# Layer B's bias rows loaded and negated one head pair earlier in a two-layer hybrid encoder

## The chip, the cores and the metric

One core of one Trainium2 chip runs the whole program. The metric is the device time of one execution in microseconds (us), the median of three runs. Each profile is of one further execution. The engines are TensorE (PE, with PEld for its weight loads), VectorE (DVE), ScalarE (ACT), GpSimd (POOL) and SyncE (SP), which here only issues DMAs.

## What is computed

The reference is a two-layer encoder block on x of shape (1, 512, 1024) in float32. Each layer is a pre-norm, one wide input projection, an attention with 16 heads of 64, a product with a gate, one output projection and a residual:

```python
hn = rms_norm(x, norm_gain[i])
if i % 2 == 0:   # layer A: three dilated windows per head, merged by their denominators
    y = mixer_a(hn, a_w_in, a_w_out, a_q_gain, a_k_gain, t5_bias)
else:            # layer B: neighbourhood attention on an 8 x 64 grid with a 2-D bias b_rpb
    y = mixer_b(hn, b_w_in, b_w_out, b_q_gain, b_k_gain, b_rpb)
x = x + y
```

In layer B a query adds to its logits `rpb[head, key row - query row + 7, key column - query column + 15]`, and a column outside its window of 16 is masked. The change is about how this table comes into the form that layer B needs; all of it is done while layer A runs.

## The kernel before

**Tiling.** Everything is kept transposed, features in the 128 partitions and the 512 tokens in the free dimension. A product runs at nearly full float32 precision as three matmuls of rounded parts (`mm3`): weights and activations are each split into a high part (`wh`, `hn_h`) and the rest (`wl`, `hn_l`). A weight piece `wraw` of 128x1024 comes from DRAM by a DMA of SP (L201) into one of four buffers; ACT or DVE rounds each half of it to `wh` (L141, L143), and POOL or DVE subtracts to get `wl` (L149, in `split`). There are four buffers each of `wh` and `wl`, and a step of a projection takes twelve matmuls for each.

**Stages.** Layer A works on the heads in eight pairs, 0 to 7. For each pair `main_a` projects keys with values (`rawk`), queries with the near keys (`rawq`), near values and the gate; after it follow the output product, then layer B in the same manner. The attention of a pair runs beside the projections of later pairs, as a generator `side()` that is pumped between matmuls. It has two halves: scores on PE into `log`, softmax on DVE (L980, L992, L826) and ACT (L1003, L827), transposes on DVE (L911) and a turn through DRAM (`td`, `pt`). The second half of pair 1 thus runs while the keys of pair 3 are projected. When ACT has copied a projection out of PSUM (L555), POOL or ACT squares it (`sq`, L315 and L313), DVE sums the squares (`ss`, L316), takes a reciprocal root (L121 to L129) and scales and turns the result (L335, L592). POOL also adds the low part of the gated output (L867).

**What sets the order.** PE's order is the program's. `clock` adds up estimated PE time while the program is written, and `later_on(delay, job)` puts a job on a list by that clock, in ns; `tick()` issues what is due. The other engines' orders are fixed when the kernel is built, by a simulated timeline in which only instructions marked `keep_in_program_order` keep their place. Every engine runs its list strictly in order, and all these DMAs stand in one list on SP.

**The bias rows of layer B.** `bias_rows()` (L467) does this:

- L470 loads `rp` (128x248, one row for each head and query row) into an `eg` buffer. There are two of these; the gates of layer A use them too (L614, L820).
- On POOL, L473 fills a second `eg` buffer `lb` (128x376) with a large number, L471 negates `rp` in place, and L474 copies its middle into `lb`.
- 16000 ns later `keep` (L476) writes both to DRAM, as `gb_d` and `lb_d` (L478).
- 30000 ns after the call, and then every 10500 ns, one of fourteen DMAs in DRAM spreads these rows into `ex_d` (L492): four of 512x160 elements, then smaller ones of 512x32 to 512x128. Four last DMAs order them into `eb_d` (L496) in pairs 4 and 5. Layer B reads `eb_d` much later.

It is called in `side()` (L1392), at the end of the first half of pair 1's attention.

Of the kernel before, what the change touches and what calls it, by code (L numbers as in the profile page):

```python
# [59 lines left out]
def tile_hybrid_encoder(  # L60
# [189 lines left out]
    def later_on(delay, job):  # L250

        timers.append((clock[0] + delay, job))
        timers.sort(key=lambda t: t[0])
# [123 lines left out]
    def row_scale(ssq):  # L377

        rsqrt(nc.vector, rs_n, ssq, 4, 1.0 / D)
# [28 lines left out]
    def gains():  # L408
        nc.sync.dma_start(hg, head_gain)
        nc.gpsimd.tensor_copy(ng.rearrange("p l k -> p (l k)"), x_ng[:, : 2 * KT])  # L410
        for i, (a, b) in enumerate(((0, 3), (1, 4), (2, 5), (6, 7))):
            m = nc.vector.scalar_tensor_tensor(
                gk[:, i : i + 1], hg[:, a : a + 1], -SCALE, hg[:, b : b + 1], op0=ALU.mult, op1=ALU.mult
            )
            tc.keep_in_program_order(m)

    def scales_a():
        pa = spread()
        nc.scalar.mul(trj(rs_half), to_trj(pa), 0.5)

    def norm(layer, k, xk):

        g = (ng if layer else x_ng[:, : 2 * KT].rearrange("p (l k) -> p l k", l=2))[:, layer, k : k + 1]
        h, l = hn_h[:, k, :], hn_l[:, k, :]
        nc.scalar.activation(h, xk, AF.Copy, scale=g)
        return nc.vector.scalar_tensor_tensor(l, xk, g, h.bitcast(F32), op0=ALU.mult, op1=ALU.subtract)

    def square_a(k):
        nc.scalar.activation(x_of(k), x_of(k), AF.Square)

    def row_sums(ssq):

        pk = bank("pk")
        for t in range(4):
            matmul(pk[:, t : t + 1], ssq[:, P * t : P * t + P], ones.bitcast(F32)[:, 0:1], start=True, stop=True)
        return pk[:, 0:4]

    def bias_lines():

        t5 = wk.tile([16, LINE], F32, tag="tr", name="t5", bufs=1)  # L440
        tc.keep_in_program_order(nc.sync.dma_start(t5, t5x))
        mk = wk.tile([16, LINE], F32, tag="q12", name="mk", bufs=1)
        nc.sync.dma_start(mk, maskc)
        nc.vector.tensor_sub(mk, mk, t5)
        nc.sync.dma_start(line_d[:, :384], mk[:, :384])
        nc.sync.dma_start(lines_d.rearrange("h g c -> h (g c)"), mk[:, 384:])

        def spread_out(dst, src):
            tc.keep_in_program_order(nc.sync.dma_start(dst, src))

        line = lambda o, *dims: bass.AP(line_d.tensor, line_d.offset + o, [[448, 16], *dims])
        fars = lambda o, *dims: bass.AP(lines_d.tensor, lines_d.offset + o, [[448, 32], *dims])
        far = l12_d.rearrange("h g r c -> (h g) r c")
        jobs = [
            (l0_d[:, 32 * j + 8 * s : 32 * j + 8 * s + 8, :], line(127 - j - 4 * s, [-16, 8], [1, 256]))
            for j in range(4)
            for s in range(4)
        ]
        jobs += [
            (far[:, 8 * s : 8 * s + 8, 56 * k : 56 * k + 56], fars(64 * (3 - s + k) + 7, [-1, 8], [1, 56]))  # L460
            for s in range(4)
            for k in range(4)
        ]
        for n, job in enumerate(jobs):
            later_on(3000 + 500 * n, partial(spread_out, *job))

    def bias_rows():  # L467

        rp = wk.tile([P, 248], F32, tag="eg", name="rp")
        tc.keep_in_program_order(nc.sync.dma_start(rp, rpb))  # L470
        nc.gpsimd.tensor_scalar(rp, rp, -1.0, None, op0=ALU.mult)  # L471
        lb = wk.tile([P, 376], F32, tag="eg", name="lb")
        nc.gpsimd.memset(lb, BIG)  # L473
        nc.gpsimd.tensor_copy(lb[:, 15 * 8 : 31 * 8], rp[:, 7 * 8 : 23 * 8])  # L474

        def keep():  # L476
            for dst, src in ((gb_d, rp), (lb_d, lb)):
                tc.keep_in_program_order(nc.sync.dma_start(dst, src))  # L478

        later_on(16000, keep)  # L480

        far, near = (lb_d, 376), (gb_d, 248)
        jobs = [(2 * W5 + W5 * n, W5, far, 120) for n in range(4)]
        jobs += [(o, 32, far, 24) for o in (0, W5, 7 * W5 - 32, 8 * W5 - 32)]
        jobs += [(32, 32, near, 216), (64, 96, near, 120), (W5 + 32, P, near, 88)]
        jobs += [(6 * W5, P, near, 56), (7 * W5, 96, near, 56), (7 * W5 + 96, 32, near, 24)]

        def spread_out(o, n, src, at):
            t, width = src
            dst = bass.AP(ex_d.tensor, ex_d.offset + o, [[4 * EB, P], [EB, 4], [1, n]])  # L490
            src = bass.AP(t.tensor, t.offset + at, [[width, P], [-8, 4], [1, n]])
            tc.keep_in_program_order(nc.sync.dma_start(dst, src))  # L492

        def in_order(c):
            dst = eb_d.rearrange("h (c r) x -> c h r x", c=4)[c]
            tc.keep_in_program_order(nc.sync.dma_start(dst, ex_d[:, c].rearrange("(h r) x -> h r x", h=16)))  # L496

        for n, job in enumerate(jobs):
            later_on(30000 + 10500 * n, partial(spread_out, *job))
        st["rows"] = [partial(in_order, c) for c in range(4)]  # L500

    st = {}
# [682 lines left out]
    def residual(src, f0):  # L1185
        xs = pq.rearrange("p (k t) -> p k t", k=KT)
        st["xr"] = [xs[:, f, :] for f in range(KT)]
        for f in range(f0, f0 + 4, 2):
            nc.sync.dma_start(xs[:, f : f + 2, :], src[:, f : f + 2, :])
            yield 1000  # L1190
# [169 lines left out]
    def side():  # L1360
        for k in range(KT):
            norm(0, k, x_of(k))
            if k:
                square_a(k - 1)
            stamp["na", k] = 0
            if k == 4:
                gains()
            yield 1000
        square_a(KT - 1)
        for k in range(1, KT):  # L1370
            yield 1300
            nc.vector.tensor_add(x_of(0), x_of(0), x_of(k))
        yield 1500
        row_scale(row_sums(x_of(0)))
        yield 2500
        bias_lines()
        later_on(21000, lambda: st.__setitem__(("e", 0), bias_a(0)))
        yield 2500
        scales_a()
        first_out()  # L1380
        stamp["rs", "a"] = 0
        halves = []
        for hc in range(NHC):
            if hc < NHC - 1:
                yield from q_a(hc)
                if hc:
                    yield from halves.pop(0)
                yield from st.pop(("land", hc))()
                half = attn_a(hc)
                for v in half:  # L1390
                    if v == "half":
                        if hc == 1:  # L1392
                            bias_rows()
                        if hc in (4, 5):
                            for n in range(2):
                                later_on(9000 + 3500 * n, st["rows"].pop())
                        halves.append(half)
                        break
                    yield v
            else:  # L1400
                gap[0] = cycle((500, 500, 700))
                yield from halves.pop(0)
                yield from chain(q_a(hc), k_a(hc))
                yield from attn_a(hc)
        yield from residual(xg, 0)
        yield from residual(xg, 4)
        stamp["ya", KT - 1, "y"] = 0
        yield "wait", ("x", KT - 1), 800
        for f in range(KT):
            square_b(f)  # L1410
            yield 600
        yield 4500
        row_scale(row_sums(st.pop("ssq")))
        stamp["rs", "b"] = 0
        yield 5000
        nc.scalar.mul(rs_half, spread(), 0.5)
        stamp["rs", "all"] = 0
        for job, hc, delay in B_PLAN:
            yield "wait", ("b", "start"), delay
            if job == "scores":  # L1420
                yield from side_b(hc)
                continue
            if hc == NHC - 1:
                yield "wait", ("back", hc), 0
                yield from residual(xm_d, 0)
            yield "wait", ("back", hc), 3500
            if hc == NHC - 2:
                stamp["yb", "turned"] = 0
            pending.pop(0)()
            if hc == NHC - 1:  # L1430
                stamp["yb", "last"] = 0
            yield
            if hc == NHC - 1:
                yield from residual(xm_d, 4)

    run(main(), side())


# [101 lines left out]
```

## Time and profile before

| | |
|---|---|
| median of 3 runs | 803.38 us (802.29 to 803.6) |
| the profiled execution | 803.4 us, of which the profiled span is 801.6 us |
| PE busy | 795.8 us, 99% of the span |
| DVE, ACT, POOL busy | 66%, 55%, 28% |
| DMA | 174.76 MB, mean 218 GB/s |

The profile covers the span; 1.8 us of the execution lie around it. Its engine rows are in us from the span's start, each with the start, the length, the engine and line, the operation, the tile written and the tiles read, the count and, in square brackets, how long the engine had been idle before and what released it. Matmuls are pipelined: one of 128x512 shows 0.39 us, but they start some 0.23 us apart. PE's granted clock is full in every slice.

### The profile page before, as it was taken

What the parts mean: (1) busy time and instruction counts of PE and PEld (TensorE: products, weight loads), DVE (VectorE), ACT (ScalarE), POOL (GpSimd) and SP (SyncE); (2) the same over time, 40 slices, a digit from 0 to 9 for tenths busy, and PEclk for the clock granted to TensorE, in tenths of its full rate; (3) what the DMA queues carried; (4) which work ended last, traced back from release to release, by engine and by line L of the source; (5) the groups of instructions that cost most, each with busy time, mean ns of one, the idle gap of its engine ahead of it and who ended that gap; (6) DMA issues with size and microseconds to landing.
All of it is one profiled execution on the core that took longest, in us unless ns stands there. A gap on an engine that the chain in (4) does not pass through costs nothing.

```text
span 801.6 us, 17757 instructions
## 1 busy us (share of the span) xinstructions
PE 795.8 (99%) x6718; PEld 654.1 (82%) x6718; DVE 526.2 (66%) x1409; ACT 442.1 (55%) x933; POOL 223.2 (28%) x351
## 2 busy tenths in 40 slices
PE   9999999999999999999999999999999999999998
PEld 7888888887888888888888888888888888887887
DVE  7474575668467568468368568538655878796744
ACT  7442744744754654664564575636336666656721
POOL 3242432441532432432532322211220405120010
PEclk9999999999999999999999999999999999999999
DMA  8579577867987986986987966166546797899564
GB/s 293 153 212 259 162 224 223 249 189 232 285 258 201 274 244 197 278 264 229 270 233 249 287 199 186 31 203 228 157 147 201 208 241 217 226 253 279 154 153 176
DMA packets 97526, 174.76 MB, mean 218 GB/s; under 512 B 16608, under 2 KB 52592, under 8 KB 97440
## 3 DMA queue, kind: packets, MB, share of 16 engines
q1 hardware_dynamic: 97296, 173.36, 74.0%
q8 instruction: 53, 0.87, 0.5%
q14 instruction: 33, 0.27, 0.1%
q10 hardware_dynamic: 144, 0.26, 0.1%
HBM read 130.98 MB, written 50.86 MB: 227 GB/s over the span
## 4 chain that ended last, share of the span: by engine, by line
PE 75%; ACT 0%; DVE 0%; issue 0%
PE acc L237 66%; PE log L237 4%; PE o L237 4%; PE tp L241 1%; ACT wh L141 0%; PE pa L237 0%; PE pk L237 0%; DVE pt L1210 0%
## 5 line engine op out<-in xcount | busy, mean ns | idle before, releaser
L237 PE MATMUL acc<-wh,hn_h 128*128 128x512 f32 x704 | 278.0, 396 | 0.9 <-ACT wh L141 0.9
L237 PE MATMUL acc<-wl,hn_h 128*128 128x512 f32 x704 | 274.0, 390 | 0.9 <-POOL wl L149 0.9
L237 PE MATMUL acc<-wh,hn_l 128*128 128x512 f32 x704 | 273.8, 390 | 0.0
L141 ACT CAST wh<-wraw 128x512 fp32r<-128x512 f32 (+1 forms) x258 | 157.7, 614 | 195.9 <-PE acc L237 161.7
L149 DVE TENSOR_TENSOR wl<-wraw,wh 128x512 fp32r<-128x512 f32 (+2 forms) x187 | 136.6, 732 | 150.8 <-ACT wh L141 149.0
L237 PEld LDWEIGHTS acc<-wh,hn_h 128*128 128x128 f32 x704 | 132.6, 188 | 32.6 <-issue 3.8
L149 POOL TENSOR_TENSOR wl<-wraw,wh 128x512 fp32r<-128x512 f32 (+1 forms) x72 | 96.1, 1335 | 225.3 <-ACT wh L141 163.8
L237 PEld LDWEIGHTS acc<-wh,hn_l 128*128 128x128 f32 x704 | 132.2, 188 | 27.7
L237 PEld LDWEIGHTS acc<-wl,hn_h 128*128 128x128 f32 x704 | 132.3, 188 | 27.5 <-POOL wl L149 1.2
L315 POOL TENSOR_TENSOR sq<-rawq 128x256 f32<-128x256 f32 (+1 forms) x82 | 59.6, 735 | 124.7 <-ACT rawq L555 112.0
L237 PE MATMUL acc<-y,wh 128*128 128x512 f32 (+1 forms) x272 | 81.6, 384 | 0.0
L1003 ACT ACTIVATE p<-p,mn 128x512 f32<-128x512 f32 (+1 forms) x64 | 44.8, 702 | 62.0 <-DVE mn L992 62.0
L237 PE MATMUL acc<-hn_h,wh 128*128 128x512 f32 x192 | 76.0, 396 | 0.0
L237 PE MATMUL acc<-hn_h,wl 128*128 128x512 f32 x192 | 74.9, 390 | 0.0
L237 PE MATMUL acc<-hn_l,wh 128*128 128x512 f32 x192 | 74.9, 390 | 0.0
L316 DVE TENSOR_REDUCE ss<-sq 128x4 f32<-128x256 f32 (+1 forms) x96 | 47.6, 505 | 34.5 <-POOL sq L315 34.0
L237 PEld LDWEIGHTS acc<-y,wh 128*128 128x128 f32 x272 | 48.9, 189 | 9.2 <-issue 0.6
L237 PE MATMUL acc<-y,wl 128*128 128x512 f32 (+1 forms) x136 | 51.4, 378 | 0.0
L335 DVE TENSOR_TENSOR rawq<-rawq,rs 128x256 f32<-128x256 f32 (+1 forms) x96 | 47.0, 550 | 2.5 <-POOL rs L133 2.2
L911 DVE STREAM_TRANSPOSE tr<-p 128x512 f32<-128x512 f32 x56 | 38.9, 705 | 11.4 <-ACT p L827 11.4
L555 ACT ACTIVATE rawq<-acc,rs_n 128x512 f32<-128x512 f32 (+1 forms) x76 | 46.0, 613 | 0.5
L827 ACT ACTIVATE p<-p,mn 128x512 f32<-128x512 f32 (+1 forms) x64 | 44.4, 701 | 2.1 <-DVE mn L826 2.1
(140 smaller groups left out, 907.8 us busy)
## 6 DMA issues: line engine op xcount, KB each, us to landing
wraw<-in_w SPq DMA_DIRECT2D x120, 512.0 KB, 5.6
td<-tr SPq DMA_DIRECT2D x14, 1024.0 KB, 7.9
pt<-td SPq DMA_DIRECT2D x56, 256.0 KB, 4.6
qd<-rawq SPq DMA_DIRECT2D x7, 1536.0 KB, 7.1
qt<-qd SPq DMA_DIRECT2D x28, 384.0 KB, 6.5
tdb<-tb SPq DMA_DIRECT2D x8, 768.0 KB, 5.7
pt<-tdb SPq DMA_DIRECT2D x32, 192.0 KB, 6.0
eb<-eb_d SPq DMA_DIRECT2D x32, 160.0 KB, 4.9
```

What stands on the lines that cost most here:

```text
L141: nc.scalar.copy(h, raw)
L149: eng.tensor_sub(l, raw, h.bitcast(F32))
L237: nc.tensor.matmul(o, l, r, **kw)
L241: nc.tensor.transpose(o, i, ident)
L315: nc.gpsimd.tensor_mul(to, v, v)
L316: nc.vector.tensor_reduce(ss[:, i * ns : (i + 1) * ns], sq.rearrange("p (a b) -> p a b", b=64), axis=AX.X, op=ALU.add)
L335: m = nc.vector.tensor_mul(v, v, by)
L555: nc.scalar.activation(dst, src, AF.Copy, scale=rs_n[:, i : i + 1])
L827: nc.scalar.activation(pr, pr, AF.Copy, scale=mn[:, 3:4])
L911: nc.vector.transpose(dst, src[:, :n].rearrange(order, b=4, k=32, **({"g": 2} if apart else {})))
L1003: nc.scalar.activation(row, row, AF.Exp, bias=mn[:, 1:2], scale=-1.0, accum_out=mn[:, 2:3])
```

## The change

`bias_rows()` is no longer called at the end of the first half of pair 1, but put on the list 12500 ns after the end of the first half of pair 0. The two writes to DRAM follow 9000 ns after the call in place of 16000, and the fourteen spreading DMAs begin 74000 ns after it in place of 30000, with the same spacing. The last four are where they were. No instruction is added or taken away.

```diff
-        later_on(16000, keep)
+        later_on(9000, keep)
...
-            later_on(30000 + 10500 * n, partial(spread_out, *job))
+            later_on(74000 + 10500 * n, partial(spread_out, *job))
...
-                        if hc == 1:
-                            bias_rows()
+                        if hc == 0:
+                            later_on(12500, bias_rows)
```

PE, DVE and ACT run the same instructions in the same order as before; rows move on POOL and SP alone. The first place is POOL's list in the first half of pair 1's attention, before: `lb` and `rp` are the bias rows, `wl` the low part of weights, `sq` the squares of pair 2's queries, `y` the gated output of pair 0.

```order
L133 TENSOR_TENSOR rs<-rs,na 128x16
L149 TENSOR_TENSOR wl<-wraw,wh 128x512
L473 MEMSET lb 128x376
L471 TENSOR_SCALAR rp<-rp 128x248
L474 COPY lb<-rp 128x128
L149 TENSOR_TENSOR wl<-wraw,wh 128x512
L315 TENSOR_TENSOR sq<-rawq 128x4x4x32 x2
```

And the same place after:

```order
L133 TENSOR_TENSOR rs<-rs,na 128x16
L149 TENSOR_TENSOR wl<-wraw,wh 128x512 x2
L315 TENSOR_TENSOR sq<-rawq 128x4x4x32 x2
L149 TENSOR_TENSOR wl<-wraw,wh 128x512
L867 TENSOR_TENSOR y<-gt,y 128x512
```

The three rows are gone from between the two `wl`, so the second `wl` and the squares no longer stand behind them. The second place is POOL's list one pair earlier, in the first half of pair 0, after; before, the same rows stood there without L473, L471 and L474.

```order
L149 TENSOR_TENSOR wl<-wraw,wh 128x512
L473 MEMSET lb 128x376
L471 TENSOR_SCALAR rp<-rp 128x248
L149 TENSOR_TENSOR wl<-wraw,wh 128x512
L474 COPY lb<-rp 128x128
L315 TENSOR_TENSOR sq<-rawq 128x4x4x32 x2
L149 TENSOR_TENSOR wl<-wraw,wh 128x512 x2
```

Here they stand ahead of one `wl` and of the squares of pair 1's queries. The third place is SP's list at the same time, after: `td` is the write of the first half's weights to DRAM, `pt` the reads of it, `vd` and `vv` the near values' turn.

```order
L201 DMA wraw<-in_w 128x1024 x3
L470 DMA rp<-in_rpb 128x248
L920 DMA td<-tr 128x4x512
L201 DMA wraw<-in_w 128x1024
L924 DMA pt<-td 32x4x512 x4
L201 DMA wraw<-in_w 128x1024
L478 DMA gb_d<-rp 128x248
L478 DMA lb_d<-lb 128x376
L201 DMA wraw<-in_w 128x1024
L644 DMA vd<-vv 128x4x128
```

Before, in pair 1, the load of `rp` stood directly behind the write of `td`; now, in pair 0, it stands directly ahead of it. The two writes stood in pair 1 between the write and the reads of `qd`, the queries' turn through DRAM. They stand now among the weight loads of pair 0.

The fourteen spreading DMAs keep their order on SP but come some places earlier: the first stood in pair 1 behind the reads of `qd` and the write of `td`, and stands now between the write `vd` and the reads `vv`, ahead of the write of `qd`.

## The prediction

> **What bounds the kernel now.** The page says it in two lines:
>
> ```profile
> span 801.6 us, 17757 instructions
> PE 795.8 (99%) x6718; PEld 654.1 (82%) x6718; DVE 526.2 (66%) x1409; ACT 442.1 (55%) x933; POOL 223.2 (28%) x351
> ```
>
> PE is busy for all but 5.8 us. The change takes no work from PE, so all it can win is one of these gaps. The waits of PE and the windows say where they are:
>
> ```profile
> PE acc L237 <- ACT wh L141: 0.9, 1, 0.9
> PE acc L237 <- POOL wl L149: 0.9, 1, 0.9
> 190.00:200.00 10.00, 8.27 (x36) 6.31 (x35) 7.48 (x15) 6.29 (x13) 2.93 (x4) 1.00 0.89 260
> 220.00:300.00 80.00, 80.00 (x742) 66.10 (x741) 51.87 (x122) 45.67 (x85) 27.11 (x38) 1.00 0.85 243
> 400.00:500.00 100.00, 100.00 (x1031) 82.17 (x1014) 73.12 (x207) 59.37 (x116) 29.42 (x33) 1.00 0.79 234
> ```
>
> Each wait row has the total, the count and the longest; a window has first its length, then PE's busy time. Between start and tail there is one hole, 1.73 us between 190 and 200 us. Matmuls are drawn longer than their spacing, so its true price comes from a repeating mark: the scores of the second half of pairs 0, 1, 2 and 3 on PE.
>
> ```profile
> 121.50 0.66 PE L237 MATMUL log<-k,q 64*32 64x256 f32 x16
> 182.99 0.66 PE L237 MATMUL log<-k,q 64*32 64x256 f32 x16
> 246.77 0.66 PE L237 MATMUL log<-k,q 64*32 64x256 f32 x16
> 308.25 0.66 PE L237 MATMUL log<-k,q 64*32 64x256 f32 x16
> ```
>
> They are 61.49, 63.78 and 61.48 us apart: the hole costs 63.78 - 61.49 = 2.29 us, 0.29% of the execution. The timelines of PE and ACT show how it ends:
>
> ```profile
> 192.90 0.39 PE L237 MATMUL acc<-wh,hn_l 128*128 128x512 f32 x1
> 194.16 0.49 PE L237 MATMUL acc<-wh,hn_h 128*128 128x512 f32 x1 [0.88 <-ACT wh L141]
> 195.51 0.50 PE L237 MATMUL acc<-wl,hn_h 128*128 128x512 f32 x1 [0.85 <-POOL wl L149]
> 192.28 1.32 ACT L827 ACTIVATE p<-p,mn 128x512 f32<-128x512 f32 x2
> 193.51 2.16 ACT L141 CAST wh<-wraw 128x512 fp32r<-128x512 f32 x4
> 194.19 1.27 POOL L149 TENSOR_TENSOR wl<-wraw,wh 128x512 fp32r<-128x512 f32 x1 [1.56 <-DMA qd<-rawq]
> ```
>
> At a spacing of 0.23 us PE wanted `wh` at 193.13 and `wl` at 193.36. ACT rounds `wh` only when pair 1's softmax is through (L827), so PE gets it at 194.16, and POOL's `wl`, done at 195.46, at 195.51. The late work is the softmax. It waited for DVE, and DVE had waited for POOL:
>
> ```profile
> 167.49 1.37 POOL L471 TENSOR_SCALAR rp<-rp 128x248 f32<-128x248 f32 x1 [11.03 <-DMA rp<-in_rpb]
> 169.18 1.29 POOL L149 TENSOR_TENSOR wl<-wraw,wh 128x512 fp32r<-128x512 f32 x1
> 170.42 1.04 POOL L315 TENSOR_TENSOR sq<-rawq 128x512 f32<-128x512 f32 x1
> 171.50 1.28 DVE L316 TENSOR_REDUCE ss<-sq 128x8 f32<-128x512 f32 x2 [3.33 <-POOL sq L315]
> 187.01 0.38 DVE L980 CUSTOM_DVE_ANT_0 p<-log,e 128x256 f32<-128x256 f32 x1
> ```
>
> POOL stood 11 us at the load of `rp`, with a `wl` and the squares queued behind it. The first square came at 170.42, DVE was idle for 3.33 us, and its timeline has hardly a gap after that until the softmax at L980 in which to catch up.
>
> **The change, part by part.** *Pair 1 loses the three POOL rows.* Pair 2 is the measure of what that gives: it has the same rows in this stretch, on each engine in the same order but for two casts of ACT (below), and no `rp`.
>
> ```profile
> 228.51 1.59 POOL L149 TENSOR_TENSOR wl<-wraw,wh 128x512 fp32r<-128x512 f32 x1 [8.62 <-ACT wh L141]
> 232.00 1.04 POOL L315 TENSOR_TENSOR sq<-rawq 128x512 f32<-128x512 f32 x1 [1.90 <-ACT rawq L555]
> 248.64 0.38 DVE L980 CUSTOM_DVE_ANT_0 p<-log,e 128x256 f32<-128x256 f32 x1
> ```
>
> Against the marks (182.99 and 246.77) the first square is 14.77 us early in pair 2 and 12.57 in pair 1, 2.20 late; L980 is 1.87 us behind its mark in pair 2 and 4.02 in pair 1, 2.15 late. So without `rp` pair 1's L980 should begin at 182.99 + 1.87 = 184.86. From L980 to the cast are 193.51 - 187.01 = 6.50 us of pair 1's own order, which the change leaves: 191.36. Then `wl` on POOL ends 2.15 us earlier, at 193.31, against 193.36 wanted. The stall just goes, with no margin; I leave 0.1 us of it. Its bounds are nothing gained, if L980 does not move, and 2.29. I take 2.2, since pair 2 is the same work.
>
> *Pair 0 gets them.* What counts is when `rp` lands. It is issued between these two:
>
> ```profile
> 100.19 0.33 SPq L201 DMA_DIRECT2D wraw<-in_w  x1
> 100.77 0.38 SPq L920 DMA_DIRECT2D td<-tr  x1
> wraw<-in_w SPq DMA_DIRECT2D x1, 512.0 KB, 4.3
> rp<-in_rpb SPq DMA_DIRECT2D x1, 124.0 KB, 7.7
> td<-tr SPq DMA_DIRECT2D x1, 1024.0 KB, 10.9
> ```
>
> The last three give the size and the time to landing: of that weight load, of `rp` before, directly behind a `td` of 1 MB, and of the slowest `td` of this stretch, issued at 196.09. Issued at about 100.6, `rp` now has only the weight load ahead, so it should land soon after 100.19 + 4.3 = 104.5: I take 104.9, between 104.5 and 100.6 + 7.7 = 108.3. POOL and DVE have there:
>
> ```profile
> 106.74 1.04 POOL L315 TENSOR_TENSOR sq<-rawq 128x512 f32<-128x512 f32 x1 [2.18 <-ACT rawq L555]
> 111.16 0.69 DVE L149 TENSOR_TENSOR wl<-wraw,wh 128x512 fp32r<-128x512 f32 x1 [0.17 <-ACT wh L141]
> 113.45 0.76 DVE L631 TENSOR_TENSOR vv<-acc,rs_half 128x448 f32<-128x448 f32 x2 [0.61 <-PE acc L237]
> 128.90 1.30 POOL L149 TENSOR_TENSOR wl<-wraw,wh 128x512 fp32r<-128x512 f32 x1 [0.34 <-DMA qd<-rawq]
> 131.64 0.39 PE L237 MATMUL acc<-wh,hn_h 128*128 128x512 f32 x1
> ```
>
> After the landing come 1.37 for the negation, 1.29 for the `wl` that now stands behind it and 0.3 for the copy to `lb`, 2.96 together: the first square starts at about 107.9 in place of 106.74, 1.1 us late. Its cover: DVE's idle 0.17 and 0.61 on the way, and at the end `wl` ready at 130.20 where PE asks for it one matmul after 131.64, at 131.87, 1.67 us. That is 2.45 us in all, so pair 0 costs nothing while `rp` lands before 106.74 + 2.45 - 2.96 = 106.2. At 108.3 it would cost 2.1 us. The `wl` behind the negation is not the first to be missed: with four buffers it is made about three steps of twelve matmuls, 8 us, ahead of its use.
>
> [...]
>
> ```profile
> 111.77 0.17 DVE L121 TENSOR_SCALAR nv<-ss 128x32 f32<-128x32 f32 x1
> 175.20 1.56 DVE L121 TENSOR_SCALAR nv<-ss 128x32 f32<-128x32 f32 x1
> 175.13 1.59 POOL L867 TENSOR_TENSOR y<-gt,y 128x512 fp32r<-128x512 f32 x1 [0.51 <-ACT y L864]
> ```
>
> So a DVE instruction can lose 1.4 us to a POOL instruction. [...] The trace agrees: the long row ends at 176.76, POOL's at 176.72. [...]
>
> *The DMAs.* Their count is the same. The two writes to DRAM no longer follow `qd` in pair 1; in pair 0 they go out among weight loads. The fourteen spreading DMAs come a few places earlier on SP. In the two full windows quoted first they ran at many places and PE missed nothing, so I put 0. The gate of pair 1 takes the buffer of `rp` again and must now wait until that is written out:
>
> ```profile
> 115.55 0.87 SPq L644 DMA_DIRECT2D vd<-vv  x1
> 135.87 0.68 DVE L613 TENSOR_TENSOR gt<-gt,rs_half 128x512 f32<-128x512 f32 x1
> ```
>
> The write stands ahead of `vd` on SP; with 7.7 us to land, as `rp` had, it is out by 123.3, and ACT writes that buffer after L613, at 136.5: 0.
>
> *Sum.* 803.4 - 2.2 + 0 = 801.2 us, of which 1.8 us lie outside the span. The profiled execution equals the median of 803.38, so the forecast stands for the median too. About 0.2%, 1.6 us, is what a measurement of this kernel can tell from no change, so that faster means below 801.8.
>
> **The rivals.** *Part of the stall stays.* The margin is 0.05 us, because in pair 1's order on ACT both last L827 stand ahead of the cast, where pair 2 has casts between them, and that order does not change. If DVE gains not 2.15 but 0.5 to 1.5 us, 0.6 to 1.6 us of stall remain: 801.8 to 802.8, no difference to be told. For: ties of DVE with POOL as above may fall otherwise. Against: pair 2.
>
> *It does nothing.* The lag of pair 1 comes from elsewhere and `rp` only happened to stand there: 803.4. Against: first square and L980 are late by the same amount.
>
> *The stall moves to pair 0.* `rp` lands 7 to 7.7 us after its issue, held up by the `td` that starts 0.2 us behind it: 1.4 to 2.1 us come back, 802.6 to 803.3.
>
> *Slower.* The same place, with a landing like the slowest `td`: 10.9 us, at 111.5. The first square would be 111.5 + 2.96 - 106.74 = 7.7 us late, PE would lose 7.7 - 2.45 = 5.3, and the time would be 803.4 - 2.2 + 5.3 = 806.5. It decides at a landing after about 110.1, 9.5 us after issue, where the loss passes 2.2 + 1.6. Against: that `td` had four reads of `qd` ahead of it; here the weight load of 4.3 us is all.
>
> **How the numbers follow.** Chances: the forecast 0.67, part of the stall 0.17, nothing 0.04, moved to pair 0 0.07, slower 0.05. The forecast's own range is 800.9 to 801.7. The range given goes from 800.8 to 802.8: it takes in the first two, 0.84, and leaves out the others. Of the forecast 0.02 may fall short of 1.6 us: faster 0.65, same 0.02 + 0.17 + 0.04 + 0.07 = 0.30, slower 0.05.
>
> **What would show it.** Right: no hole in PE between 190 and 200 us; marks 61.5 us apart for pairs 1 and 2; L980 of pair 1 some 1.9 us behind its mark; POOL's negation at about 105 and the first square of pair 0's stretch before 109.2. Wrong in pair 1: L980 still 3 us or more behind its mark. Wrong in pair 0: a hole in PE at about 131.6 with L471 later than 106.2. A new hole elsewhere, behind a weight load delayed by an `ex_d`, would make the zero for the DMAs wrong.

## The result, and the profile after

The changed kernel takes 801.35 us (median of 12 runs, 801.1 to 802.38) where the kernel before takes 803.5 us (12 runs beside it, 802.29 to 804.89). The ratio is 0.9973 with a 95% interval of 0.9964 to 0.9982: faster by 0.27%, some 2.15 us. The forecast was 801.2 us.

The profiled execution of the changed kernel took 802.38 us, the slowest of the twelve; its page begins like that of before:

```profile
span 800.6 us, 17757 instructions
PE 795.9 (99%) x6718; PEld 653.9 (82%) x6718; DVE 526.8 (66%) x1409; ACT 442.3 (55%) x933; POOL 222.2 (28%) x351
```

PE does the same 795.9 us of work, but its gaps are now 800.6 - 795.9 = 4.7 us in place of 5.8. The waits of PE (total, count, longest) and the windows say which one went:

```profile
PE busy L401 <- DVE warm L390: 0.9, 1, 0.9
PE o L237 <- DVE mn L826: 0.6, 1, 0.6
190.00:200.00 10.00, 10.00 (x45) 8.04 (x45) 5.09 (x8) 5.88 (x12) 3.20 (x4) 1.00 0.72 169
400.00:500.00 100.00, 99.44 (x1012) 81.58 (x1011) 72.34 (x202) 58.84 (x114) 29.28 (x33) 1.00 0.79 230
```

The two waits on `wh` and `wl` at 193 to 195.5 us are gone, and the window from 190 to 200 is full. A small one is new, at 463 us; the run `again` below deals with it. The same repeating marks as before, the scores of the second half of pairs 0 to 3:

```profile
121.58 0.66 PE L237 MATMUL log<-k,q 64*32 64x256 f32 x16
183.08 0.66 PE L237 MATMUL log<-k,q 64*32 64x256 f32 x16
244.75 0.66 PE L237 MATMUL log<-k,q 64*32 64x256 f32 x16
306.25 0.66 PE L237 MATMUL log<-k,q 64*32 64x256 f32 x16
```

They are 61.50, 61.67 and 61.50 us apart, against 61.49, 63.78 and 61.48. The middle distance lost 2.11 us, which is the result but for some hundredths. The first did not grow: pair 0 pays nothing for what it took over. The middle one is still 0.17 us longer than its neighbours, and PE's timeline shows where:

```profile
193.22 0.39 PE L237 MATMUL acc<-wh,hn_h 128*128 128x512 f32 x1
193.47 0.50 PE L237 MATMUL acc<-wl,hn_h 128*128 128x512 f32 x1
193.80 0.39 PE L237 MATMUL acc<-wh,hn_l 128*128 128x512 f32 x1
```

The matmul that needs POOL's `wl` starts 0.25 us after the one ahead of it, and the next 0.33 us after that, in place of 0.23 each. The last matmul of the old stall had the same look (0.50 long, the next one 0.34 behind it). So a rest of the stall is still there, too short for the list of waits.

The timelines of POOL, DVE and ACT show pair 1 after:

```profile
164.83 1.59 POOL L149 TENSOR_TENSOR wl<-wraw,wh 128x512 fp32r<-128x512 f32 x1 [8.62 <-ACT wh L141]
168.32 1.04 POOL L315 TENSOR_TENSOR sq<-rawq 128x512 f32<-128x512 f32 x1 [1.90 <-ACT rawq L555]
169.39 1.44 DVE L316 TENSOR_REDUCE ss<-sq 128x8 f32<-128x512 f32 x2 [1.13 <-POOL sq L315]
184.94 0.38 DVE L980 CUSTOM_DVE_ANT_0 p<-log,e 128x256 f32<-128x256 f32 x1
190.22 1.32 ACT L827 ACTIVATE p<-p,mn 128x512 f32<-128x512 f32 x2
191.44 1.65 ACT L141 CAST wh<-wraw 128x512 fp32r<-128x512 f32 x3
192.12 1.29 POOL L149 TENSOR_TENSOR wl<-wraw,wh 128x512 fp32r<-128x512 f32 x1 [1.57 <-ACT wh L141]
```

POOL's idle time of 11.03 us on the load of `rp` is gone. What it waits for now is the queries themselves: 1.90 us, ended by ACT's copy out of PSUM, the very bracket that pair 2 showed before. From there every row is some 2.1 us earlier against the mark: the first square 14.76 ahead of it in place of 12.57, L980 1.86 behind it in place of 4.02, the cast 8.36 behind it in place of 10.52.

Pair 0 after, on SP, POOL and DVE; the fourth row is the load's size and its time to landing:

```profile
100.26 0.33 SPq L201 DMA_DIRECT2D wraw<-in_w  x1
100.64 0.42 SPq L470 DMA_DIRECT2D rp<-in_rpb  x1
101.16 0.38 SPq L920 DMA_DIRECT2D td<-tr  x1
rp<-in_rpb SPq DMA_DIRECT2D x1, 124.0 KB, 4.5
105.25 0.83 POOL L471 TENSOR_SCALAR rp<-rp 128x248 f32<-128x248 f32 x1 [7.23 <-DMA rp<-in_rpb]
106.05 1.29 POOL L149 TENSOR_TENSOR wl<-wraw,wh 128x512 fp32r<-128x512 f32 x1
107.28 0.76 POOL L474 COPY lb<-rp 128x128 f32<-128x128 f32 x1
108.00 1.04 POOL L315 TENSOR_TENSOR sq<-rawq 128x512 f32<-128x512 f32 x1
```

POOL stands here too, for 7.23 us, and the first square begins at 108.00. Measured from the issue of the weight load (100.26, before 100.19) that is 7.74 us, against 106.74 - 100.19 = 6.55 before: 1.19 us late, and no gap in PE follows.

### The profile page after: what moved, and what is told of

Its sections match the earlier page's. It is cut to its first block, busy times and chain, and to the rows that moved or that the text cites. A ratio compares the mean times of both kernels' runs of the same rounds, so it can differ in the third digit from the quotient of the medians.

```text
span 800.6 us, 17757 instructions
## 1 busy us (share of the span) xinstructions
PE 795.9 (99%) x6718; PEld 653.9 (82%) x6718; DVE 526.8 (66%) x1409; ACT 442.3 (55%) x933; POOL 222.2 (28%) x351
## 4 chain that ended last, share of the span: by engine, by line
PE 90%; DVE 5%; DMA 3%; ACT 2%; issue 1%; ACTq 0%; SPq 0%
PE acc L237 79%; PE log L237 4%; PE o L237 4%; DMA vv<-vd 1%; DVE rawq L335 1%; DMA bd<-rawq 1%; PE tp L241 1%; DVE wl L149 1%; DMA wraw<-in_w 1%; PE busy L401 1%; ACT wh L141 0%; ACT p L1300 0%; DVE na L128 0%; ACT p L1305 0%; DVE rawq L592 0%
```

## The experiments

**Theory W**, the prediction's: the 2.1 us are the wait of POOL at the load, with the squares of pair 2 queued behind it; in pair 0 the same wait is covered. **Rival D**: what counts are the DMAs that left pair 1, above all the two writes behind `qd`. **Rival R**: the work of the three rows itself counts in pair 1, through POOL's time or through DVE held up beside it.

**`rows_only`.** From the kernel before. The load goes to pair 0, into a buffer of its own. `bias_rows` is still called in pair 1, so that the two writes and the spreading DMAs stay there; POOL's rows go to pair 0 with the load, by the order that is fixed when the kernel is built (the negation runs at 105.00).

```diff
+    def load_rows():
+        st["rows6"] = slot(6, "rows6", F32)
+        st["rp"] = st["rows6"][:, :248]
+        tc.keep_in_program_order(nc.sync.dma_start(st["rp"], rpb))
...
-        rp = wk.tile([P, 248], F32, tag="eg", name="rp")
-        tc.keep_in_program_order(nc.sync.dma_start(rp, rpb))
+        rp = st["rp"]
-        lb = wk.tile([P, 376], F32, tag="eg", name="lb")
+        lb = st["rows6"][:, 256:632]
...
+                        if hc == 0:
+                            later_on(12500, load_rows)
```

> The load of rp and the three POOL rows go to pair 0 as in the changed kernel; the two writes of gb_d and lb_d and the fourteen spreading DMAs stay where the kernel before has them (the rows stand in a buffer of their own, so that no gate waits for it). Theory W (POOL's wait at the load of rp, with the squares behind it, made pair 1's softmax late): 801.2 to 801.5 us, the whole gain, pair 1's mark to pair 2's mark 61.5 to 61.7 us. Rival D (the DMA traffic around the queries' turn in pair 1, the two writes behind qd, made it late): 803.4, marks 63.8 apart, L980 of pair 1 still about 4 us behind its mark.

801.26 us (5 runs; ratio 0.9968, 0.9956 to 0.9981). The marks stand 61.49, 61.71 and 61.49 apart. The whole gain is there with the DMAs at their old places: D falls.

**`ahead`.** From the kernel before. Everything stays in pair 1; the load alone is issued some 9 us earlier, ahead of one weight load and of `td`, and the POOL rows stand one `wl` further ahead. The delays are raised so that the later DMAs keep their places.

```diff
                 later_on(7000 + 2000 * u, send)
+                if hc == 1 and u == 0:
+                    later_on(6990, bias_rows)
...
-        later_on(16000, keep)
+        later_on(19200, keep)
...
-            later_on(30000 + 10500 * n, partial(spread_out, *job))
+            later_on(33200 + 10500 * n, partial(spread_out, *job))
...
-                        if hc == 1:
-                            bias_rows()
```

> Nothing leaves pair 1: only the load of rp goes ahead of one weight load and of the write of td, and POOL's three rows ahead of one more wl; every DMA after it stands as in the kernel before. Theory W: rp lands near 156 to 160 us, POOL is through with its rows before the next weights are cast at 164.6, the first square comes near 168.3 and the stall is gone: 801.2 to 801.6 us. Rival R (the work of the three rows in pair 1, or POOL and DVE blocking each other there): stays at 803 or above. Rival D: 803.4.

801.22 us (5 runs; ratio 0.9967, 0.9954 to 0.9979), marks 61.49, 61.72 and 61.49 apart. POOL's timeline in pair 1:

```profile
157.54 0.83 POOL L471 TENSOR_SCALAR rp<-rp 128x248 f32<-128x248 f32 x1 [6.43 <-DMA rp<-in_rpb]
168.13 1.04 POOL L315 TENSOR_TENSOR sq<-rawq 128x512 f32<-128x512 f32 x1 [1.90 <-ACT rawq L555]
```

POOL still stands 6.43 us at the load, and the rows still cost POOL their time in pair 1, but the wait is over 10 us before the queries arrive. R falls, and with it any need to leave pair 1. What counted before was when POOL was through with all that stood ahead of the squares. By pair 2's measure the squares of pair 1 could start 14.77 us ahead of the mark, at 168.22. The wait ended at 167.49, a little earlier, but the negation, the copy and the `wl` queued behind it took 2.93 us more, until 170.42.

**`wait_more`.** From the kernel before, with a copy of 0.5 MB within DRAM put ahead of the load, to make the wait longer.

```diff
+        tc.keep_in_program_order(nc.sync.dma_start(dr.tile([P, 1024], F32, name="dum"), w[:, :1024]))
         tc.keep_in_program_order(nc.sync.dma_start(rp, rpb))
```

> The kernel before with one more DMA, 0.5 MB from DRAM to DRAM that nothing reads, directly ahead of the load of rp; all orders else the same. Theory W: rp lands 2 to 4 us later than 167.5 and the stall grows by as much, since pair 1 has no cover left: 805 to 808 us, the hole in PE near 193 us grows to 4 to 6 us in the distance of the marks. Rival D, and the view that rp only happened to stand there: within 0.5 us of 803.4.

805.66 us (10 runs, 803.4 to 807.31; ratio 1.0025, 1.0011 to 1.0039). POOL's negation came only some 1.4 us later against the mark, and the first square (171.06, mark 182.73) 0.90 later than before, so the dose was smaller than meant. The price was larger: the marks are 66.07 us apart, 2.29 more than before. PE's timeline, a matmul of the usual look behind it, and two windows (the third figure from the end is PE's granted clock):

```profile
194.71 0.50 PE L237 MATMUL acc<-wh,hn_h 128*128 128x512 f32 x1 [1.68 <-ACT wh L141]
196.06 0.79 PE L237 MATMUL acc<-wl,hn_h 128*128 128x512 f32 x1 [0.85 <-POOL wl L149]
196.66 0.63 PE L237 MATMUL acc<-wh,hn_l 128*128 128x512 f32 x1
199.47 0.40 PE L237 MATMUL acc<-wh,hn_h 128*128 128x512 f32 x1
193.00:197.00 4.00, 1.47 (x4) 1.01 (x4) 3.24 (x5) 3.22 (x6) 2.08 (x3) 0.85 0.76 207
197.00:201.00 4.00, 4.00 (x14) 3.13 (x13) 1.24 (x1) 0.59 (x1) 0.69 (x1) 0.72 1.05 230
```

The first of the two idle times grew from 0.88 to 1.68 us, by 0.8, about the 0.9 us of the later square, as W has it. The rest is the clock: between 196.66 and 199.22 the matmuls take 0.63 us and start 0.43 apart in place of 0.23, that is, at about half speed (granted clock 0.85 and 0.72 in the two windows), and the windows lose 4 x 0.15 + 4 x 0.28 = 1.7 us (2.5 together, a little over the 2.29 of the marks). No theory had this. The ten runs divide in the same way: the three at a mean clock of 1.000 took 803.4 to 804.26 us, the seven at 0.996 to 0.998 took 805.4 to 807.31. So W's sign and its first 0.8 us held, and that the median lies in the expected 805 to 808 us is luck: the clock made up for the dose that was too small.

**`wait_pair0`.** From the changed kernel, with a DMA of 4096 single elements ahead of the load.

```diff
+        some = bass.AP(w.tensor, w.offset, [[w.ap[0][0], P], [2, 32]])
+        tc.keep_in_program_order(nc.sync.dma_start(dr.tile([P, 32], F32, name="dum"), some))
         tc.keep_in_program_order(nc.sync.dma_start(rp, rpb))
```

> The changed kernel with one more DMA of 4096 single elements, from DRAM to DRAM and read by nothing, directly ahead of the load of rp in pair 0; on POOL the wl goes ahead of the negation. My cover of 2.45 us in pair 0: time is 801.35 plus the first square's delay beyond 106.8 + 2.45 = 109.3 us, nothing if the square starts before that. With a landing 5 to 15 us later than 105.2 that makes a hole in PE near 131.7 us and 803 to 815 us. Rival: pair 0 has other slack (or none), so that the hole differs from that difference by over 0.5 us.

842.33 us (4 runs, 838.86 to 847.48). The dose was far too large, as SP's and PE's timelines show:

```profile
101.67 23.93 SPq L922 DMA_DIRECT2D td<-tr  x1
158.59 0.80 PE L237 MATMUL acc<-hn_h,wl 128*128 128x512 f32 x1 [41.59 <-POOL wl L149]
```

SP could not issue the next DMA for 24 us, and the first square came at 154.37. It shows that pair 0 can pay for the wait; taken alone it says little about how much is covered.

**`td_ahead`.** From the changed kernel, with a copy of 512 bytes ahead of the load; the order built for SP then has `td` between the two, so the load stands behind 1 MB as it did in pair 1. POOL's negation and copy come behind the next `wl`.

```diff
+        tc.keep_in_program_order(nc.sync.dma_start(dr.tile([1, 128], F32, name="dum"), w[:1, :128]))
         tc.keep_in_program_order(nc.sync.dma_start(rp, rpb))
```

> The changed kernel, with one copy of 512 bytes within DRAM put ahead of the load of the bias rows; the scheduler then issues the write of the scratch behind the small copy and ahead of the load, so the load stands behind that write of 1 MB as it did in pair 1 of before. Nothing of the result changes. Landing by that place's row in before (7.7 us after the issue, here at some 102.1): 109.8 in place of 105.2; the next weight half now stands ahead of the negation, so 0.83 and 0.76 us of POOL follow and the first square begins at some 111.4, 4.6 us behind the mark of before where the changed kernel has 1.2. Theory of the prediction (2.45 us of cover in pair 0): a stall of about 2.1 us there, 803.5 us. Rival 'no cover, every microsecond of the squares counts': 1.2 is paid already, so 3.4 more, 804.7. Rival 'the wait in pair 0 lies beside slack and never counts': 801.3.

801.21 us (6 runs; ratio 0.9971, 0.996 to 0.9982), not the 803.5 of the theory. POOL's timeline says why:

```profile
107.56 0.84 POOL L472 TENSOR_SCALAR rp<-rp 128x248 f32<-128x248 f32 x1 [2.70 <-DMA rp<-in_rpb]
108.46 0.29 POOL L475 COPY lb<-rp 128x128 f32<-128x128 f32 x1
108.72 1.04 POOL L315 TENSOR_TENSOR sq<-rawq 128x512 f32<-128x512 f32 x1
```

The load, issued at 102.10, was there after 5.4 us and not 7.7, and the copy took 0.29. The first square is 1.69 us late by the measure used above, still under 2.45, so this run can't decide between the cover and the rival for which the wait in pair 0 never counts. The rival for which every microsecond counts falls: the mark of pair 1 came no later (table below).

**`dose_1`, `dose_2`, `dose_4`.** The same with 128, 256 and 512 single elements in place of the 512 bytes, to push the first square past the cover.

```diff
+        some = bass.AP(w.tensor, w.offset, [[w.ap[0][0], P], [2, 1]])
+        tc.keep_in_program_order(nc.sync.dma_start(dr.tile([P, 1], F32, name="dum"), some))
         tc.keep_in_program_order(nc.sync.dma_start(rp, rpb))
```

> As the run with the small copy, but the copy is of 512 single elements, with the write of the scratch between it and the load again. By the run with 4096 elements (load landed 48.0 us later than in the changed kernel, some 4.6 of it by its place behind the write, so 10.6 ns for each element) the load lands 5.4 us later than with the small copy, at about 115.2, and the first square begins at 116.8, 10.0 us behind the mark. Cover theory: 10.0 - 2.45 = 7.5 us of stall, 808.9 us. No cover: 801.35 + 8.8 = 810.2. Never counts: 801.3. What is looked at: the stall of PE against the lateness of the first square, which should go up one for one beyond 2.45.

> As the run with 512 single elements ahead of the load (and the write of the scratch between), with 128. Between the small copy and 512 elements the load landed 7.2 us later by equal starts, 14 ns for each element, so here 1.8 later: at about 109.0, the first square at 110.1, 3.4 us behind the mark. Theory of the prediction (2.45 us of cover, by L980 and the casts behind it): 0.95 of stall at about 131.6, 802.2 us. Rival 'the first thing to be late is the weight half behind the squares, which has 5.2 us of cover (by the run with 512 elements: 8.8 late, a hole of 3.45), and L980 is not late': no stall, 801.2.

> The same with 256 elements: the load lands at about 110.8, the first square begins at 111.9, 5.2 us behind the mark. Theory of the prediction (2.45 us of cover): 2.75 of stall at about 131.6, 804.0 us; if TensorE's granted clock halves behind a hole of that length as it did behind 3.3 us, up to 2.8 more, 806.8. Rival '5.2 us of cover at the weight half behind the squares, and L980 not late': no stall, 801.2 to 801.4.

They took 807.91 us (6 runs, 805.73 to 808.52) with 128 elements, 809.03 (4 runs, 807.7 to 809.55) with 256 and 808.22 (4 runs, 807.66 to 809.58) with 512. The expected times of the two smaller doses were missed, since the load landed 10.9 and 11.9 us after its issue, and 12.5 with 512 elements; the delay does not go with the number of elements. The stall against the lateness, however, can be read from each. PE's timeline with 128 elements, and the window around its second stall:

```profile
117.82 0.50 PE L237 MATMUL acc<-hn_h,wl 128*128 128x512 f32 x1 [1.55 <-POOL wl L149]
135.08 0.50 PE L237 MATMUL acc<-wh,hn_h 128*128 128x512 f32 x1 [1.72 <-ACT wh L141]
136.43 0.50 PE L237 MATMUL acc<-wl,hn_h 128*128 128x512 f32 x1 [0.85 <-POOL wl L149]
135.00:140.00 5.00, 4.07 (x17) 3.14 (x18) 2.52 (x5) 3.44 (x7) 2.72 (x2) 1.00 0.73 157
```

The stall at 133 to 136 us is the one that the prediction named for pair 0, with the same two waits that pair 1 had before. Ahead of it a `wl` behind the squares is missed too. With 256 elements the second stall has the same two lengths, 1.69 and 0.85, but the clock behind it drops:

```profile
135.00:140.00 5.00, 2.80 (x7) 2.06 (x8) 3.35 (x6) 4.08 (x9) 2.21 (x3) 0.80 0.67 177
140.00:145.00 5.00, 5.00 (x20) 4.04 (x20) 1.29 (x2) 1.37 (x3) 0.64 (x1) 0.86 1.06 222
```

With 512 elements the first idle time is long, and the clock halves right there (two rows). The third row is of `wait_pair0`, at the place of the second stall:

```profile
119.72 0.79 PE L237 MATMUL acc<-hn_h,wl 128*128 128x512 f32 x1 [3.29 <-POOL wl L149]
119.72:123.00 3.28, 3.28 (x8) 2.60 (x9) 3.18 (x8) 0.40 (x1) 1.60 (x3) 0.50 0.65 163
177.08 0.50 PE L237 MATMUL acc<-wl,hn_h 128*128 128x512 f32 x1 [0.24 <-POOL wl L149]
```

The kernels changed in pair 0, with times counted from the issue of the weight load ahead of `td` on SP. "Late" is the first square against 6.55 us (before), "stall" the mark of pair 1 against 182.99 - 100.19 = 82.80 us (before):

| kernel | weight load | first square | mark of pair 1 | late | stall | late - stall |
|---|---|---|---|---|---|---|
| behind0 (below) | 100.02 | 106.57 | 182.82 | 0.00 | 0.00 | |
| changed kernel | 100.26 | 108.00 | 183.08 | 1.19 | 0.02 | |
| td_ahead | 100.48 | 108.72 | 183.30 | 1.69 | 0.02 | |
| dose_1 | 99.86 | 113.59 | 187.70 | 7.18 | 5.04 | 2.14 |
| dose_2 | 100.08 | 114.86 | 190.55 | 8.23 | 7.67 | 0.56 |
| dose_4 | 100.03 | 115.49 | 189.59 | 8.91 | 6.76 | 2.15 |
| wait_pair0 | 100.60 | 154.37 | 228.34 | 47.22 | 44.94 | 2.28 |

`rows_only`, by the same measure, is 1.03 us late with a stall of 0.01. Up to 1.69 us late nothing is paid; from 7.18 on all is paid but 2.1 to 2.3 us, in a range from 7 to 47 us. Between 1.69 and 7.18 there is no run. The odd one, with 256 elements, lost 5 x 0.20 + 5 x 0.14 = 1.7 us to the clock after its second stall, and 0.56 + 1.7 = 2.3 again. In `dose_4` and `wait_pair0` PE is slow ahead of the second stall (granted clock 0.50 from 119.72 in `dose_4`, matmuls 0.43 us apart from 159.18 to 163.88 in `wait_pair0`), and there it costs nothing on top. By the mark of pair 0 (127.73 and 166.31, before 121.50) PE is already 6.39 and 44.40 us late there, so that it comes to the second place only just before the late `wl`, and no more than 0.37 and 0.54 us are added. PE still stands at that `wl`, for 0.24 us in the row above, so it is the late softmax that sets the total. So the wait in pair 0 does count, and the cover is about 2.2 us. The rival for which it never counts falls, and so does the one with 5.2 us of cover.

**`behind0`.** From the changed kernel; the rows are put on the list 6 us later, so that the load goes out among the reads `pt` and POOL's negation and copy stand behind the squares.

```diff
-                            later_on(12500, bias_rows)
+                            later_on(18500, bias_rows)
```

> The changed kernel with the three rows given to the planner 6 us later in pair 0: the load is issued behind three of the reads of the averaged scratch, and POOL's negation and copy stand behind the two squares, so nothing that the path needs stands behind the wait. Theory of the prediction (the 1.2 us that the first square is late lies within the cover and costs nothing): 801.3 us, the same as the changed kernel within 0.3, and the square back at about 106.8. Rival 'pair 0 pays for the wait unseen': faster than the changed kernel by up to 1.2, some 800.2. Rival 'the load is now queued behind the reads and delays the gates of pair 0': slower, 802 or more.

801.13 us (5 runs, 800.95 to 801.39; ratio 0.9968, 0.9956 to 0.9981). POOL's timeline:

```profile
106.57 1.04 POOL L315 TENSOR_TENSOR sq<-rawq 128x512 f32<-128x512 f32 x1 [1.83 <-ACT rawq L555]
113.25 0.84 POOL L471 TENSOR_SCALAR rp<-rp 128x248 f32<-128x248 f32 x1 [2.42 <-DMA rp<-in_rpb]
```

The square is 1.19 us earlier than in the changed kernel and the time the same within what the runs can tell. The lateness that the change accepts in pair 0 costs nothing.

**`again`.** The changed kernel once more, for a second profile.

> The changed kernel once more, nothing altered, for a second profile. The first one (802.38 us, the slowest of its twelve runs) shows a hole of 1.0 us in PE at 462.6, at the values of pair 5, which wait for reads of the scratch that landed late. If that hole belongs to the change it is there again, of about 1 us, and the time is near 802.4; if it varies from run to run, as 0.2 us in the run with the rows alone and none in the others suggest, it is smaller or gone here and the time near 801.3. The stall at 190 to 200 us stays gone in both.

801.43 us, span 799.7. In the first profile PE's timeline has the values of pair 5 late:

```profile
462.63 0.44 PE L237 MATMUL o<-pt,rawk 64*64 64x128 f32 x4
463.63 1.40 PE L237 MATMUL o<-pt,rawk 64*64 64x128 f32 x55 [0.56 <-DVE mn L826]
450.96 4.09 SPq L924 DMA_DIRECT2D pt<-td  x4
```

In the second profile there is no wait of PE but the one at the start, and those four reads went out at 449.90, 1.06 us earlier, though the write ahead of them had been issued at the same time within 0.1 us. So this hole of about 1 us varies from one execution to the next of the same kernel. It would explain why the profiled run was the slowest, 1.03 us over the median. That the later reads made it is likely and not tested; whether the kernel before can show it too, its one profile can't tell.

## Why the prediction was right

- **The bound.** The one hole in PE was the gain: marks 63.78 us apart became 61.67, and `rows_only`, `ahead`, `td_ahead` and `behind0` end at 61.67 to 61.72. The prediction left 0.1 us of stall. What stays is 0.17 to 0.23 in every kernel, whether the rows are in pair 1 or not, and it lies at the matmul that needs `wl`, as shown above for the changed kernel. So the rest that the prediction feared is real, but small; the term of 2.2 us is 2.11.
- **The chain through POOL, DVE and ACT.** First square, L980 and cast were forecast at 2.20, 2.15 and 2.15 us earlier against the mark; they came 2.19, 2.16 and 2.16 earlier. Taking pair 2 as the measure of pair 1 without the rows held row by row. L980 was to begin 1.87 us behind its mark and began 1.86 behind it. `wl` on POOL ended at 193.41 in place of 193.31, and PE wanted it at 193.22 + 0.23 = 193.45. In the old stall 0.05 us lay between the end of `wl` (195.46) and PE's start (195.51), so that this is just too late: the tie that the prediction feared cost most of the 0.17 us.
- **Pair 0's landing.** Forecast 104.9, with bounds of 104.5 and 108.3. POOL began the negation at 105.25, the load 4.5 us after its issue. Two smaller terms were off and cancel, by luck: the negation took 0.83 and not 1.37, the copy 0.76 and not 0.3, so that 2.75 us lie from the negation to the first square where 2.96 were forecast, and the square began at 108.00 where 107.9 was forecast.
- **Pair 0's cover.** Forecast 2.45 us, put together from two idle times of DVE and the slack of one `wl`. The doses give 2.1 to 2.3. The place was right, a second stall on `wh` and then `wl` once the square is too late, and so were the parts. DVE's timeline has L980 with 512 elements, where it is line 982, and before:

```profile
131.03 0.38 DVE L982 CUSTOM_DVE_ANT_0 p<-log,e 128x256 f32<-128x256 f32 x1
122.95 0.38 DVE L980 CUSTOM_DVE_ANT_0 p<-log,e 128x256 f32<-128x256 f32 x1
```

  From the weight load it is (131.03 - 100.03) - (122.95 - 100.19) = 8.24 us late where the first square was 8.91 late, so DVE made up 0.67 of its 0.78 us, and 8.24 - 6.76 = 1.48 stand against the 1.67 at the end. What the prediction did not name is the first `wl` behind the squares, which is missed when the square is about 5.3 us late: with 128 elements PE's mark in pair 0 is 1.89 us late at 7.18 us of lateness.
- **DVE beside POOL.** DVE lost time beside the moved rows. The first two rows are DVE's after, beside them; the third is the first of these instructions before:

```profile
106.07 1.82 DVE L149 TENSOR_TENSOR wl<-wraw,wh 128x512 fp32r<-128x512 f32 x1 [2.12 <-ACT wh L141]
109.08 1.28 DVE L316 TENSOR_REDUCE ss<-sq 128x8 f32<-128x512 f32 x2 [1.19 <-POOL sq L315]
105.99 0.69 DVE L149 TENSOR_TENSOR wl<-wraw,wh 128x512 fp32r<-128x512 f32 x1 [2.12 <-ACT wh L141]
```

  It took 1.82 us in place of 0.69, 1.13 us more, beside a `wl` of POOL that ran from 106.05 to 107.34; before, POOL was idle from 104.56 to 106.74, all the while that it ran. The prediction's rows of L121 show a like loss: the same instruction took 0.17 us in pair 0, where POOL was idle, and 1.56 in pair 1, where it ended 0.04 us behind POOL's row. That POOL's rows held DVE up is an inference from these times; what the two contend for, no run shows. In pair 0 it cost nothing: DVE was ahead there, and was idle for 1.19 us after it until the square came. So the forecast, which has no term for it, was the right one.
- **The DMAs at 0.** Right: `rows_only`, with the DMAs at their old places, and the changed kernel, with all of them moved, differ by 0.09 us.

**The rivals.** "Part of the stall stays" and "does nothing" fell with the marks. "The stall moves to pair 0" and "slower" rested on a later landing; the doses show that the mechanism is real, with a slope of one to one beyond 7 us, and that with the load there by 105.25 it was not reached. Of "part of the stall stays" the 0.17 us are true.

## What to carry to other kernels

On POOL the rows behind a wait stood with it: pair 1's `wl` began at 169.18 behind the load, and at 164.83 without it. Yet the length of the wait at the DMA did not by itself set the price: 6.43 and 7.23 us cost nothing, 11.03 us cost 2.1. What counted was whether the wait, and the work queued between it and the instruction that the path needs, ended after that instruction could have started, by more than the path has to spare. So ask of each wait not how long it is but what is queued behind it and when that is ready. Moving the load 9 us up in the same pair was worth as much as moving it all a pair earlier, and so was putting the waiting rows behind the squares in pair 0; none of these beat another.

A stage that repeats gives the measure: the same rows in the next pair, against a mark on the bound engine, forecast each row of the chain within about 0.1 us.

## What had not been expected of the hardware

**A short stall can cost clock as well.** After idle times of 3.29 us (`dose_4`) and 41.59 us (`wait_pair0`) PE's matmuls of 128x512 started 0.43 us apart in place of 0.23 for 5.1 and 4.7 us (granted clock 0.50 in the window of `dose_4` shown), and after 1.68 and 0.85 us with one matmul between them (`wait_more`) for 2.6 us. Nearly the same two idle times came without the drop in the run with 128 elements (1.72 and 0.85 us, clock 1.00) and with it in the run with 256 (1.69 and 0.85 us, 0.80 and 0.86); there one idle time of 2.61 us, the first stall, came without it (clock 1.00 from 115 to 125). It varies between executions too: of the six runs with 128 elements, two at a mean clock of 1.000 took 805.73 and 805.98 us, and four at 0.998 took 807.79 to 808.52. The kernel before seems to have it: of the 35 runs of it that were measured beside the experiments, the ten at 0.998 took 804.62 to 805.0 us and all others 801.94 to 803.82. No run of the changed kernel is under 0.999, nor one of `rows_only`, `ahead`, `td_ahead` and `behind0`, 34 runs in all. So, as an estimate from these times, the stall of 2.1 us most likely cost some 1.5 us more in more than one run of four, and the change took that away as well. That the clock of those runs fell at this stall is an inference: the one profile of before is at full clock. What decides whether the clock drops, no run shows; by the runs with 128 and 256 elements it is not the length of the idle times alone.

**Single elements were dear in the queue.** In these runs the copy and the write of `td` went out ahead of the load. Behind a copy of 512 bytes in one row of 128 elements, which itself landed after 3.3 us, the load landed 5.4 us after its issue. Behind 128 single elements, also 512 bytes, which landed after 9.5 us, it landed after 10.9; behind 512 elements after 12.5. With 4096 SP needed 23.93 us to issue the DMA after it. Nothing between the one row and 128 single elements was tried.
